# Pinned background sums, gate rows by way of memory, softmax normalization on ScalarE, and value products of two column blocks in one visit

## The chip, the cores and the metric

The kernel runs on one core of a Trainium2 chip. The metric is the device time of one execution in microseconds (us). The core has five engines that the profile tells apart: PE (TensorE, the matmuls, with the weight loads PEld that overlap them), DVE (VectorE), ACT (ScalarE), POOL (GpSimd) and SP (SyncE, which here only issues DMAs). Each engine works through its own queue of instructions in order and waits at an instruction until what that needs is there.

## The reference

Two layers of a diffusion backbone, for 1024 latent tokens of a 16 x 64 grid and 256 context tokens, width 1024. One input projection feeds three branches; their outputs are joined, projected, gated and normalized.

```python
shift, scale, gate = split(silu(c) @ w_mod + b_mod, 3)     # and the same for the context, from c_ctx
h = x * (1 + scale) + shift
p = h @ w_in                                               # cut into rk rv nk nv rq rg nq ng ch cb ccg cz
y = concat([conv(ch, cb, ccg, cz),                         # 4 groups, width-3 filter
            retention(rq, rk, rv) * silu(rg),              # 6 heads x 64, both directions
            neighbourhood(nq, nk, nv) * silu(ng)]) @ w_out # 6 heads x 64
x = layer_norm(ALPHA * x + gate * y)
# neighbourhood, for one latent query: a window of 8 rows x 16 columns and all 256 context keys
s = concat([q . k_window + bias, q . k_ctx]);  o = softmax(s) @ [v_window, v_ctx]
```

Context queries see context keys only, and layer 1 has no context queries.

## The kernel before

**Numbers.** Projections are made in two parts: a tensor is cut into a rounded part and a rest (tiles wh and wl of the weights, h of the activations; KS holds both parts of the keys, QH and QL are the query's), and PE multiplies the parts that matter. All such products go through the helper mm at L86, transposes through L140.

**The order of the work.** PE's order is written out by the program. A class Order keeps a clock od.t, to which every matmul adds its cost; generators that run beside the main line (the attention of a column block, the background sums, the load of the output weights) yield a number and are resumed when the clock has gone on by that much, between two matmuls of a projection. The other engines' orders are made by a scheduler from what each instruction needs and from its priority, which is its place in the program; `behind(60)` (L206) puts the background sums 60 places back, but the scheduler may still put them ahead of an instruction recorded earlier if that one's data come later.

**The background sums.** Mod.background (L189 to L227) makes the modulation's shift, scale and gate columns for later use: tiles wm of w_mod come in by DMA (SP), DVE multiplies them by silu(c) and adds them up in acc (L210 the first, L212 the others, two versions: latent and context), PE transposes acc, DVE sums the transposed columns and adds the bias into the table `tab` (L183). In layer 0 it makes that layer's gate (four groups of columns) and then the shift and scale of layer 1 (eight); in layer 1 only that layer's gate. The job is called `aside` and runs beside the attention branch.

**The attention branch** goes in three column blocks of two heads (p = 0, 1, 2) in each layer, six cores in all. For each, the keys are projected (ps_pj, evacuated into KS by ACT at L659 and by DVE at L660, the rest), POOL builds bias tables B (L715, L720), the queries are projected, and then the generator core (L726 to L817) runs beside the next projections. An item is 128 queries of one head: 4 context items (layer 0 only) and 16 latent ones for each core. One step of the loop at L788 does three things for three different items:

- scores of item `step`: PE makes them into one or two ps_s banks; DVE takes the maximum of the context part (m, L753), adds the bias B and takes the joint maximum (mx, L756), and negates it (nm, L758); ACT takes the exponential with the row sum (L760); DVE forms the reciprocal (L696) and multiplies P by it and by 0.5 (L697, normalize).
- values of an item pair at `step - LAG - 2` (LAG = 2): the two heads' PT tiles times the values VA into ps_pv (L777 to L780), a stretch of matmuls that read 128 rows and write 64 partitions, which the profile shows as tile shape 128*64 while the rest runs as 128*128. This happens at every second step; four of these blocks of 64 columns fill the one ps_pv bank, and ACT copies it out to oN (L808, L810).
- turn of the item at `step - LAG` (L764 to L775): PE transposes its P into ps_pt, ACT copies 512 columns out to PT (L770) and DVE the last 128 (L774).

```python
for step in range(n + LAG + 3):
    if step < n:
        Ps[kind, i] = s_lat(i) if kind == "l" else s_ctx(i)
    back = step - LAG - 2
    if 0 <= back < n and items[back][1] % 2 == 1:
        pv(ov[:, c * 128:(c + 1) * 128], vals, pair)
    back = step - LAG
    if 0 <= back < n:
        PTs[kind, i] = turn(Ps.pop((kind, i)), nt)
    yield (1800 if p < 2 else 1500) if step < n else 800
```

PSUM has eight banks: 3 for ps_pj, 2 for ps_s, 2 for ps_pt and 1 for ps_pv. There are three buffers each for P and PT.

**The end of a layer.** After the third core, w_out (L1070) loads the output weights (SP, 16 loads, L1080) and splits them (ACT L1081, DVE L1082). The gate is a column table (128 partitions), but is needed as a row in every partition: gate_rows (L1050) multiplies the identity by table columns into dg (DVE, L1055) and multiplies dg by a matrix of ones on PE into two ps_s banks; gate_copy (L1064) copies these to gt (ACT, L1067). That happens once for the latent tokens in each layer, and once more for the context in layer 0, beside the sixth tile of the output loop (L1110).

Of the kernel before, what the change touches and what calls it, by code (L numbers as in the profile page):

```python
# [30 lines left out]
LAG = 2  # L31
# [48 lines left out]
def backbone(ctx: ExitStack, tc: tile.TileContext, io):  # L80
# [43 lines left out]
    ones = const.tile([128, 128], F, name="c_ones")  # L124
    dve.memset(ones, 1.0)
# [19 lines left out]
    class Mod:  # L145
# [43 lines left out]
        def background(self, blocks, tmp):  # L189
# [10 lines left out]
            for i, (blk, kk) in enumerate(todo):  # L200
                if i + 2 < len(todo):
                    tiles.append(load(*todo[i + 2]))
# [3 lines left out]
                with behind(60):  # L206
                    for v in range(2):
                        c = cs[:, kk, v:v + 1]
                        if kk == 0:
                            dve.tensor_scalar(acc[:, v], t, c, None, ALU.mult)  # L210
                        else:
                            dve.scalar_tensor_tensor(acc[:, v], t, c, acc[:, v],  # L212
                                                     ALU.mult, ALU.add)
# [415 lines left out]
    def natten_conv(l, h, yT, vn, ctx_q, aside, w_out):  # L629
# [3 lines left out]
        with ExitStack() as st:  # L633
# [60 lines left out]
            def normalize(P, n, s):  # L694
                r = col("rc1")
                dve.reciprocal(r, s)  # L696
                dve.tensor_scalar(P[:, :n], P[:, :n], r, 0.5, ALU.mult, ALU.mult)  # L697
# [28 lines left out]
            def core(p, QH, QL, KS, bias, oN):  # L726
# [37 lines left out]
                def turn(P, nt):  # L764
                    PT = np_.tile([128, 640], F, tag="PT", bufs=3, name="PT")
# [4 lines left out]
                    act.copy(PT[:, :n], pt[:, :n])  # L770
                    if nt > 4:
                        pt = ps_t()
                        transpose(pt[:, :128], P[:, 512:640])
                        dve.tensor_copy(PT[:, 512:640], pt[:, :128])  # L774
# [13 lines left out]
                for step in range(n + LAG + 3):  # L788
# [5 lines left out]
                    back = step - LAG - 2  # L794
                    if 0 <= back < n and items[back][1] % 2 == 1:
                        kind, i = items[back]
                        k = i // 2
                        pair = [PTs.pop((kind, i - 1)), PTs.pop((kind, i))]
                        vals = [VA[:, a, :] for a in (8, 9)]
                        if kind == "l":  # L800
                            k0, nt = window(k)
                            vals += [VA[:, a, :] for a in range(k0, k0 + nt)]
                        c = k % 4
                        if c == 0:
                            ov = ps_v()
                        pv(ov[:, c * 128:(c + 1) * 128], vals, pair)
                        if kind == "c" and k == 1:
                            act.copy(oN[:, SEQ:TOK], ov[:, :256])  # L808
                        elif kind == "l" and c == 3:
# [224 lines left out]
    for l in range(DEPTH):  # L1034
        last = l == DEPTH - 1
        yT = dram.tile([DM, TOK], F, name=f"yT{l}")
        vn = [dram.tile([TOK, 128], F, name=f"vn{l}{p}") for p in range(3)]
        mod_l = mod
        mod_n = None if last else Mod(l + 1)

        def aside(tmp):
            yield from mod_l.background(range(16, 24, 2), tmp)
            if mod_n is not None:
# [3 lines left out]
        with ExitStack() as st:  # L1047
            wo, held, op, job = [], [], None, None

            def gate_rows(v, held):  # L1050

                for hf in range(2):
                    ps = ps_s()
                    dg = const.tile([128, 512], F, tag="m2", name="dg")
                    dve.tensor_tensor(  # L1055
                        dg.rearrange("p (j c) -> p j c", c=128),
                        ident.unsqueeze(1).to_broadcast([128, 4, 128]),
                        mod_l.tab[:, 16 + 4 * hf:20 + 4 * hf, v:v + 1]
                        .to_broadcast([128, 4, 128]), ALU.mult)
                    yield 8000  # L1060
                    mm(ps, ones, dg, True, True, 866)
                    held.append(ps)

            def gate_copy(held):  # L1064
                gt = op.tile([128, DM], F, tag="gt", name="gt")
# [185 lines left out]
```

## Time and profile before

| | us |
|---|---|
| median of 3 runs | 1394.04 (1393.85 to 1395.64) |
| the profiled execution | 1394.43 |
| its span, first to last instruction | 1392.7 |
| PE busy in it (PEld 1161.9) | 1360.6, 98% |
| DVE busy | 945.5, 68% |
| ACT busy | 475.9, 34% |
| POOL busy | 320.4, 23% |

The granted TensorE clock is 0.997 of full speed over the whole span. The profile holds a page (busy time of each engine, the span in slices, the chain of work that ended last, the costliest groups of instructions) and a trace from which rows can be asked: the waits of an engine, the timeline of a stretch, busy time in windows. A row of the timeline gives the start, the duration, the engine, the program's line, the operation, out<-in by tile names, shapes, and how many like instructions it stands for; in square brackets the idle time ahead of it and who ended that. PE records are kept for a part of a long product at times as one, so counts of PE rows ("shown matmuls") are those of the trace.

### The profile page before, as it was taken

The page shows a single profiled execution, that of the slowest core. Times are in us where ns is not written, and L with a number is a line of the kernel's source. Part 1 is how long each engine was busy: PE and PEld are TensorE (multiplying, and loading weights), DVE is VectorE, ACT ScalarE, POOL GpSimd, SP SyncE. Part 2 cuts the span into 40 slices and gives each one's busy share as a digit, 9 for nine tenths or more (in the row PEclk, how much of TensorE's full clock was granted, in tenths as well). Part 3 has the DMA queues.
Part 4 walks back from the last instruction along what each step waited for, and adds up shares of the span by engine and source line. Part 5 has one row for each costly group of instructions (what it writes and reads, how often), then busy time and mean ns, then how long its engine had stood idle before and what let it go on. Part 6 is the DMA issues. An engine that isn't in the chain of part 4 may idle for free.

```text
span 1392.7 us, 23906 instructions
## 1 busy us (share of the span) xinstructions
PE 1360.6 (98%) x9040; PEld 1161.9 (83%) x9040; DVE 945.5 (68%) x2331; ACT 475.9 (34%) x1000; POOL 320.4 (23%) x266
## 2 busy tenths in 40 slices
PE   6999999998999999999999999999999999999997
PEld 4888989887888888888888888888878888887886
DVE  4766473638887877875988766565489756465686
ACT  2422122223453443543344422121234435354210
POOL 1505041341021121000444404041440213100121
PEclk9999999999999999999999999999999999999999
DMA  9720201233113224126343211111252211203642
GB/s 291 225 58 16 58 24 33 71 108 112 54 58 121 86 63 126 43 82 215 133 133 117 83 49 33 48 34 55 69 152 61 74 56 46 80 24 98 197 153 89
DMA packets 160788, 126.31 MB, mean 91 GB/s; under 512 B 10272, under 2 KB 146080, under 8 KB 160672
## 3 DMA queue, kind: packets, MB, share of 16 engines
q1 hardware_dynamic: 160672, 124.78, 29.6%
q8 instruction: 71, 1.16, 0.3%
q14 instruction: 45, 0.37, 0.1%
HBM read 102.98 MB, written 21.76 MB: 90 GB/s over the span
## 4 chain that ended last, share of the span: by engine, by line
PE 86%; DVE 7%; DMA 2%; issue 2%; SPq 1%; ACT 1%; POOL 0%; POOLq 0%; DVEq 0%; ACTq 0%
PE ps_pj L86 66%; PE ps_s L86 7%; PE ps_pt L140 7%; PE ps_pv L86 6%; DVE acc L212 2%; DMA wm<-in_w_mod 2%; PE ps_pt L86 1%; DVE P L756 1%; DVE P L697 1%; DVE KS L660 0%; DVE P L753 0%; DVE sm L424 0%; SPq L157 0%; DMA rs<-in_ropes 0%; DVE rsw L397 0%
## 5 line engine op out<-in xcount | busy, mean ns | idle before, releaser
L86 PE MATMUL ps_pj<-h,wh 128*128 128x512 f32 (+1 forms) x2128 | 624.7, 373 | 6.7 <-DVE KS L660 4.6
L86 PEld LDWEIGHTS ps_pj<-h,wh 128*128 128x128 f32 x2128 | 379.3, 189 | 68.0 <-issue 7.0
L86 PE MATMUL ps_pj<-h,wl 128*128 128x512 f32 (+1 forms) x1064 | 395.6, 372 | 0.0
L86 PEld LDWEIGHTS ps_pj<-h,wl 128*128 128x128 f32 x1064 | 201.5, 189 | 32.1 <-issue 2.9
L86 PE MATMUL ps_pj<-wo,yh 128*128 128x512 f32 (+1 forms) x608 | 182.7, 382 | 0.0
L86 PE MATMUL ps_pj<-wh,h 128*128 128x256 f32 x960 | 175.2, 284 | 1.3 <-ACT nv L430 1.3
L86 PEld LDWEIGHTS ps_pj<-wh,h 128*128 128x128 f32 x960 | 150.5, 192 | 2.0 <-ACT nv L430 1.5
L86 PE MATMUL ps_pj<-wl,h 128*128 128x256 f32 x480 | 136.4, 284 | 0.0
L86 PEld LDWEIGHTS ps_pj<-wo,yh 128*128 128x128 f32 x608 | 112.0, 188 | 21.7 <-issue 1.0
L212 DVE SCALAR_TENSOR_TENSOR acc<-wm,c_silu,acc 128x256 f32<-128x256 f32 x224 | 117.5, 563 | 2.6 <-DMA wm<-in_w_mod 2.2
L86 PE MATMUL ps_pj<-wo,yl 128*128 128x512 f32 (+1 forms) x304 | 115.9, 381 | 0.0
L235 POOL TENSOR_TENSOR wl<-wr,wh 128x512 fp32r<-128x512 f32 x32 | 43.1, 1346 | 313.0 <-ACT wh L243 267.6
L243 ACT CAST wh<-wr 128x512 fp32r<-128x512 f32 x128 | 79.1, 619 | 91.2 <-PE ps_pj L86 86.9
L760 ACT ACTIVATE P<-P,nm 128x640 f32<-128x640 f32 (+1 forms) x96 | 77.3, 805 | 75.4 <-DVE nm L758 72.4
L235 DVE TENSOR_TENSOR wl<-wr,wh 128x512 fp32r<-128x512 f32 x96 | 71.3, 745 | 43.9 <-ACT wh L243 42.6
L770 ACT COPY PT<-ps_pt 128x512 f32<-128x512 f32 (+1 forms) x108 | 60.6, 561 | 101.7 <-PE ps_pt L140 101.3
L86 PEld LDWEIGHTS ps_pj<-wl,h 128*128 128x128 f32 x480 | 92.1, 192 | 0.3 <-POOL wl L235 0.2
L715 POOL TENSOR_TENSOR B<-E,c_rmask 128x256 f32<-128x256 f32 (+1 forms) x36 | 38.4, 1076 | 178.5 <-DVE mx L756 136.7
L140 PE MATMUL ps_pt<-c_ident,P 128*128 128x128 f32 x480 | 73.0, 278 | 1.7 <-DVE P L697 1.1
L422 DVE TENSOR_REDUCE sm<-ps_pj 128x2 f32<-128x128 f32 x60 | 17.3, 289 | 75.6 <-PE ps_pj L86 75.0
L86 PEld LDWEIGHTS ps_pj<-wo,yl 128*128 128x128 f32 x304 | 57.3, 188 | 11.1 <-issue 0.5
L140 PEld LDWEIGHTS ps_pt<-c_ident,P 128*128 128x128 f32 x480 | 54.5, 140 | 12.2 <-issue 7.2
(168 smaller groups left out, 2003.1 us busy)
## 6 DMA issues: line engine op xcount, KB each, us to landing
wr<-in_w_in SPq DMA_DIRECT2D x104, 256.0 KB
wm<-in_w_mod SPq DMA_DIRECT2D x128, 128.0 KB
wr<-yT SPq DMA_DIRECT2D x36, 256.0 KB
yT<-ystage SPq DMA_DIRECT2D x32, 256.0 KB
wr<-in_w_out SPq DMA_DIRECT2D x32, 256.0 KB
wm<-in_w_mod SPq DMA_DIRECT2D x12, 512.0 KB
wr<-in_w_in SPq DMA_DIRECT2D x48, 128.0 KB
z<-in_x SPq DMA_DIRECT2D x8, 512.0 KB
```

The lines of the kernel that those rows point to most:

```text
L86: pe.matmul(out, lhsT, rhs, start=start, stop=stop)
L140: pe.transpose(out, in_, ident[:in_.shape[0], :in_.shape[0]])
L212: dve.scalar_tensor_tensor(acc[:, v], t, c, acc[:, v], ALU.mult, ALU.add)
L235: eng.tensor_tensor(lo, raw, f32(hi), ALU.subtract)
L243: act.copy(hi, raw)
L422: dve.tensor_reduce(sm, ps[:, :128].rearrange("p (h d) -> p h d", d=HD), AX.X, ALU.add)
L697: dve.tensor_scalar(P[:, :n], P[:, :n], r, 0.5, ALU.mult, ALU.mult)
L715: pool.tensor_tensor(B, bass.AP(tensor=E.tensor, offset=E[:, o:o + 1].offset, ap=[list(E.ap[0]), [1, nc_], [RPB_W, 16]]), rmask.unsqueeze( ...
L756: dve.tensor_tensor_reduce(P[:, 256:256 + n], sl[:, :n], B, 1.0, m0, ALU.add, ALU.max, mx)
L760: act.activation(P[:, :256 + n], P[:, :256 + n], AF.Exp, bias=nm, accum_out=s)
L770: act.copy(PT[:, :n], pt[:, :n])
```

## The change

Four edits are made.

1. The sums of the background (L210, L212) are pinned: the scheduler keeps each in its place of the program on DVE, so that it goes behind all DVE instructions recorded ahead of it.
2. The gate rows no longer go over PE. When the gate table is complete, SP writes its columns to a tensor gd in DRAM (one DMA of 128 x 8 single elements for each version) and later reads it back with a broadcast to 128 partitions (one DMA of 512 KB each). The products with ones, dg, the copies and the matrix of ones go. The first broadcast stands ahead of the loads of the output weights, the second (layer 0) ahead of the output loop.
3. The normalization's product moves from DVE to ACT (a Copy with the reciprocal as scale). The factor 0.5 moves to the two evacuations of the transposes.
4. The products with the values are made for two blocks of columns in one stretch, at every fourth step, and one step after the last turn of the four items and not two. PT has four buffers, and a core is two steps shorter.

```diff
-    ones = const.tile([128, 128], F, name="c_ones")
-    dve.memset(ones, 1.0)
...
                         if kk == 0:
-                            dve.tensor_scalar(acc[:, v], t, c, None, ALU.mult)
+                            i = dve.tensor_scalar(acc[:, v], t, c, None, ALU.mult)
                         else:
-                            dve.scalar_tensor_tensor(acc[:, v], t, c, acc[:, v],
-                                                     ALU.mult, ALU.add)
+                            i = dve.scalar_tensor_tensor(acc[:, v], t, c, acc[:, v],
+                                                         ALU.mult, ALU.add)
+                        tc.keep_in_program_order(i)
...
                 r = col("rc1")
                 dve.reciprocal(r, s)
-                dve.tensor_scalar(P[:, :n], P[:, :n], r, 0.5, ALU.mult, ALU.mult)
+                act.activation(P[:, :n], P[:, :n], AF.Copy, scale=r)
...
-                    PT = np_.tile([128, 640], F, tag="PT", bufs=3, name="PT")
+                    PT = np_.tile([128, 640], F, tag="PT", bufs=4, name="PT")
...
-                    act.copy(PT[:, :n], pt[:, :n])
+                    act.activation(PT[:, :n], pt[:, :n], AF.Copy, scale=0.5)
...
-                        dve.tensor_copy(PT[:, 512:640], pt[:, :128])
+                        dve.tensor_scalar(PT[:, 512:640], pt[:, :128], 0.5, None, ALU.mult)
...
-                for step in range(n + LAG + 3):
+                for step in range(n + LAG + 1):
...
-                    back = step - LAG - 2
-                    if 0 <= back < n and items[back][1] % 2 == 1:
-                        kind, i = items[back]
-                        k = i // 2
-                        pair = [PTs.pop((kind, i - 1)), PTs.pop((kind, i))]
...
-                        pv(ov[:, c * 128:(c + 1) * 128], vals, pair)
-                        if kind == "c" and k == 1:
+                    back = step - LAG - 1
+                    if 0 <= back < n and back % 4 == 3:
+                        for x in (back - 3, back - 1):
+                            kind, i = items[x]
+                            k = i // 2
+                            pair = [PTs.pop((kind, i)), PTs.pop((kind, i + 1))]
...
+                            pv(ov[:, c * 128:(c + 1) * 128], vals, pair)
+                        if kind == "c":
...
+        gd = dram.tile([2, DM], F, name=f"gd{l}")
...
             yield from mod_l.background(range(16, 24, 2), tmp)
+            for v in range(1 if last else 2):
+                sp.dma_start(gd[v].rearrange("(b p) -> p b", p=128), mod_l.tab[:, 16:24, v])
             if mod_n is not None:
...
-            def gate_rows(v, held):
-                for hf in range(2):
-                    ps = ps_s()
-                    dg = const.tile([128, 512], F, tag="m2", name="dg")
-                    dve.tensor_tensor(
...
-                    yield 8000
-                    mm(ps, ones, dg, True, True, 866)
-                    held.append(ps)
-            def gate_copy(held):
-                gt = op.tile([128, DM], F, tag="gt", name="gt")
-                for hf, ps in enumerate(held):
-                    act.copy(gt[:, hf * 512:(hf + 1) * 512], ps)
+            def gate_rows(pool, v):
+                gt = pool.tile([128, DM], F, tag="gt", bufs=1, name="gt")
+                sp.dma_start(gt, gd[v:v + 1, :].to_broadcast([128, DM]))
                 return gt
...
-                job = od.start(gate_rows(0, held))
+                gts.append(gate_rows(op, 0))
...
-            od.finish(job)
-            gt = gate_copy(held)
+            if not last:
+                gts.append(gate_rows(lp, 1))
             for t in range(8 if last else 10):
-                if t == 6 and not last:
-                    held = []
-                    job = od.start(gate_rows(1, held))
-                if t == 8:
-                    od.finish(job)
-                    gt = gate_copy(held)
+                gt = gts[t // 8]
```

The instructions on PE go from 7978 to 7972, on DVE from 2309 to 2194, on ACT from 894 to 996; SP issues 580 in place of 574.

On PE, layer 0, second column block, this is one of the steps with a visit to the values before (PT the transposed P, VA the values, c_ident the identity of the transposes); such a step is every second one:

```order
L86 MATMUL ps_s<-KS,QH 128x256
L86 MATMUL ps_s<-KS,QL 128x256
L86 MATMUL ps_s<-KS,QH 128x384
L86 MATMUL ps_s<-KS,QL 128x384
L86 MATMUL ps_pv<-PT,VA 64x128 x10
L140 MATMUL ps_pt<-c_ident,P 128x128 x5
```

The same place now, where such a step is every fourth one:

```order
L86 MATMUL ps_s<-KS,QH 128x256
L86 MATMUL ps_s<-KS,QL 128x256
L86 MATMUL ps_s<-KS,QH 128x384
L86 MATMUL ps_s<-KS,QL 128x384
L86 MATMUL ps_pv<-PT,VA 64x128 x20
L138 MATMUL ps_pt<-c_ident,P 128x128 x5
```

The stretch of value products has become twice as long and stands at half as many places, between the same neighbours; over the program there are 54 before and 27 now.

On ACT, layer 0, first column block, before (L760 the exponential, L770 the copy of the transposes, L659 the evacuation of the next keys, L810 the copy of ps_pv):

```order
L760 ACTIVATE P,sa<-P,nm 128x640
L770 COPY PT<-ps_pt 128x512
L760 ACTIVATE P,sa<-P,nm 128x640
L770 COPY PT<-ps_pt 128x512
L760 ACTIVATE P,sa<-P,nm 128x640
L659 CAST KS<-ps_pj 64x64x8
L810 COPY oN<-ps_pv 128x16x32
L770 COPY PT<-ps_pt 128x512
L760 ACTIVATE P,sa<-P,nm 128x640
L659 CAST KS<-ps_pj 64x64x8
L770 COPY PT<-ps_pt 128x512
```

The same place now, in the line numbers of the changed kernel (L759 the exponential, L696 the new product, L769 the copy, L658 the keys; rc is the reciprocal):

```order
L759 ACTIVATE P,sa<-P,nm 128x640
L696 ACTIVATE P<-P,rc_4278 128x640
L759 ACTIVATE P,sa<-P,nm 128x640
L810 COPY oN<-ps_pv 128x16x32
L696 ACTIVATE P<-P,rc_4315 128x640
L769 ACTIVATE PT<-ps_pt 128x512
L658 CAST KS<-ps_pj 64x64x8
L769 ACTIVATE PT<-ps_pt 128x512
L658 CAST KS<-ps_pj 64x64x8
L759 ACTIVATE P,sa<-P,nm 128x640
L696 ACTIVATE P<-P,rc_4384 128x640
L769 ACTIVATE PT<-ps_pt 128x512
```

A product follows each exponential in ACT's queue, at times with another instruction between, and the copies of the transposes and the casts of the keys stand behind it.

On DVE, layer 0, the first key projection, before (L660 the rest of the keys, two for each bank of ps_pj; L210 and L212 the sums):

```order
L660 TENSOR_TENSOR KS<-ps_pj,KS 64x64x8 x2
L210 TENSOR_SCALAR acc<-wm,c_silu 128x256 x2
L212 SCALAR_TENSOR_TENSOR acc<-wm,c_silu,acc 128x256 x6
L660 TENSOR_TENSOR KS<-ps_pj,KS 64x64x8
L212 SCALAR_TENSOR_TENSOR acc<-wm,c_silu,acc 128x256 x2
L660 TENSOR_TENSOR KS<-ps_pj,KS 64x64x8
L212 SCALAR_TENSOR_TENSOR acc<-wm,c_silu,acc 128x256 x2
```

The same place now (L659 the rest of the keys, L208 and L210 the sums):

```order
L659 TENSOR_TENSOR KS<-ps_pj,KS 64x64x8 x2
L208 TENSOR_SCALAR acc<-wm,c_silu 128x256 x2
L210 SCALAR_TENSOR_TENSOR acc<-wm,c_silu,acc 128x256 x6
L659 TENSOR_TENSOR KS<-ps_pj,KS 64x64x8 x2
L210 SCALAR_TENSOR_TENSOR acc<-wm,c_silu,acc 128x256 x2
L659 TENSOR_TENSOR KS<-ps_pj,KS 64x256
L210 SCALAR_TENSOR_TENSOR acc<-wm,c_silu,acc 128x256 x2
```

Eight sums still stand between the first bank's keys and the second's; the two that stood between the halves of the second bank stand behind them now.

## What the change will do to the time

> **What bounds the kernel now.** I read the page first: busy time by engine, then the chain that ended last.
>
> ```profile
> PE 1360.6 (98%) x9040; PEld 1161.9 (83%) x9040; DVE 945.5 (68%) x2331; ACT 475.9 (34%) x1000; POOL 320.4 (23%) x266
> PE 86%; DVE 7%; DMA 2%; issue 2%; SPq 1%; ACT 1%; POOL 0%; POOLq 0%; DVEq 0%; ACTq 0%
> ```
>
> PE is busy for 1360.6 of the span's 1392.7 us and holds 86% of the chain; only 32.1 us are idle. So there are two places to win: instructions that leave PE's stream, which count in full, and the idle time in which PE waits for another engine. The waits of PE tell what the second can be worth.
>
> ```profile
> PE ps_pv L86 <- DMA wm<-in_w_mod: 8.2, 6, 4.8
> PE ps_pj L86 <- DVE KS L660: 4.6, 2, 3.6
> PE ps_s L86 <- DVE m L753: 2.0, 2, 1.0
> PE ps_s L86 <- DVE mx L756: 1.9, 5, 0.6
> PE ps_pt L140 <- DVE P L697: 1.1, 1, 1.1
> PE ps_pt L140 <- DVE nm L758: 0.3, 1, 0.3
> PE ps_pt L140 <- DVE PT L774: 0.3, 1, 0.3
> ```
>
> The columns are total, times and longest, in us. The first row belongs to the kernel's first stage, which the diff leaves alone. The second is the key projection in which the background sums begin, 4.6 us. The other five lie in the attention stage and have one cause, a late VectorE: 2.0 + 1.9 + 1.1 + 0.3 + 0.3 = 5.6 us. Three windows out of the six attention cores (three column blocks in each layer) say why: one with sums in layer 0, one with sums and one without in layer 1. The columns used are window, length, then busy us of PE, PEld, DVE and ACT.
>
> ```profile
> 345.00:415.00 70.00, 68.87 (x523) 59.51 (x521) 59.53 (x191) 34.34 (x74) 10.82 (x10) 1.00 0.20 59
> 1040.00:1104.00 64.00, 61.40 (x436) 51.53 (x438) 59.75 (x183) 30.47 (x63) 11.06 (x10) 1.00 0.22 64
> 1216.00:1272.00 56.00, 55.63 (x410) 46.69 (x409) 34.91 (x128) 27.96 (x58) 2.85 (x2) 1.00 0.08 23
> ```
>
> Where background sums run beside the softmax, DVE is busy 85% (59.53 of 70.00) and 93% (59.75 of 64.00), and PE loses 1.1 and 2.6 us; ACT stands at 48 to 50%. Without sums (last row) DVE is at 62% and PE loses 0.4.
>
> **The change part by part.** *Visits to the 64-column shape.* The matmuls with the values (tiles PT and VA) run as 128*64, everything around them as 128*128. Two neighbourhoods of PE's timeline price one visit (start, length, and xcount), one without and one with it.
>
> ```profile
> 481.21 0.34 PE L86 MATMUL ps_s<-KS,QL 128*128 128x384 f32 x1
> 481.39 0.71 PE L140 MATMUL ps_pt<-c_ident,P 128*128 128x128 f32 x5
> 481.86 0.48 PE L86 MATMUL ps_pj<-h,wh 128*128 128x256 f32 x2
> ```
>
> ```profile
> 484.45 0.34 PE L86 MATMUL ps_s<-KS,QL 128*128 128x384 f32 x1
> 484.72 1.31 PE L86 MATMUL ps_pv<-PT,VA 128*64 128x128 f32 x20
> 485.96 0.77 PE L140 MATMUL ps_pt<-c_ident,P 128*128 128x128 f32 x5
> 486.48 0.71 PE L86 MATMUL ps_pj<-h,wh 128*128 128x512 f32 x2
> ```
>
> A short visit, of 8 matmuls, gives the pitch:
>
> ```profile
> 462.38 0.66 PE L86 MATMUL ps_pv<-PT,VA 128*64 128x128 f32 x8
> ```
>
> Without a visit PE goes from the last score matmul to the projection in 481.86 - 481.21 = 0.65 us; with one, in 486.48 - 484.45 = 2.03. Of the 1.38 between them the 20 matmuls themselves take 20 x 0.054 = 1.08 (pitch: (1.31 - 0.66) / 12, from the runs of 20 and 8). The visit as such costs 0.30 us. The order has 54 visits before (10 in each of layer 0's three cores, 8 in layer 1's) and 27 now, with the same matmuls: 27 x 0.30 = 8.1 us off PE. A block of the two costs nothing more for coming second, since within a visit the pitch is even.
>
> *The gate rows.* Six products with a matrix of ones, each shown as two matmuls, leave PE. One of them, with the rhythm of the same projection just ahead of it:
>
> ```profile
> 641.08 0.40 PE L86 MATMUL ps_pj<-h,wh 128*128 128x256 f32 x2
> 641.31 0.28 PE L86 MATMUL ps_pj<-h,wl 128*128 128x256 f32 x1
> 641.43 0.40 PE L86 MATMUL ps_pj<-h,wh 128*128 128x256 f32 x2
> 641.67 1.02 PE L86 MATMUL ps_s<-dg,c_ones 128*128 128x512 f32 x2
> 642.13 0.68 PE L86 MATMUL ps_pj<-h,wl 128*128 128x256 f32 x1
> 642.65 0.40 PE L86 MATMUL ps_pj<-h,wh 128*128 128x256 f32 x2
> ```
>
> A group of three takes 641.43 - 641.08 = 0.35; with the gate's two it takes 642.65 - 641.43 = 1.22. So 6 x 0.87 = 5.2 us. In their place SP issues three writes of 1024 single elements to memory and three broadcasts of 512 KB. The writes stand right behind the last gate table's sum, the first broadcast ahead of most loads of the output weights. I cost them at nothing: SP holds 1% of the chain, and weights are loaded ahead. Were that cover gone, the weight loads queued behind the write on SP would be late by its wait for the table, and PE with them once in each layer: up to 2 us, kept for the range.
>
> *Pinned sums.* On DVE the sums no longer overtake what was recorded ahead of them. The two key projections show what that is worth. DVE in layer 0:
>
> ```profile
> 311.75 1.76 DVE L210 TENSOR_SCALAR acc<-wm,c_silu 128x256 f32<-128x256 f32 x2 [1.10 <-DMA wm<-in_w_mod]
> 313.43 6.86 DVE L212 SCALAR_TENSOR_TENSOR acc<-wm,c_silu,acc 128x256 f32<-128x256 f32 x6
> 320.32 0.68 DVE L660 TENSOR_TENSOR KS<-ps_pj,KS 64x512 fp32r<-64x512 f32 x1
> 321.04 0.88 DVE L212 SCALAR_TENSOR_TENSOR acc<-wm,c_silu,acc 128x256 f32<-128x256 f32 x2
> 321.95 0.69 DVE L660 TENSOR_TENSOR KS<-ps_pj,KS 64x512 fp32r<-64x512 f32 x1
> ```
>
> The matmul on PE that waits for it, and POOL's work of the same time:
>
> ```profile
> 322.79 0.70 PE L86 MATMUL ps_pj<-h,wh 128*128 128x512 f32 x2 [3.63 <-DVE KS L660]
> ```
>
> ```profile
> 314.17 3.45 POOL L715 TENSOR_TENSOR B<-E,c_rmask 128x256 f32<-128x256 f32 x3
> ```
>
> PE's bank comes free with the fourth KS, at 321.95 + 0.69. The new order still has eight sums ahead of the third KS, but none between third and fourth: it gains 321.95 - 320.32 - 0.68 = 0.95 us here and, the order being the same, in layer 1: 1.9 us of the 4.6. The rest stays: the six sums take 6.86 / 6 = 1.14 us each, most of it while POOL builds its tables, against 0.88 / 2 = 0.44 right after, and both the six and the tables stand where they stood. If a new order brought them to 0.44, they would end 4.2 us earlier, the whole 4.6 would go, and the sum below would be 18.7 in place of 16.0; I don't take it, since nothing is moved between the six and the tables. [...]
>
> *Normalization on ScalarE.* DVE loses 108 products, ACT gains them.
>
> ```profile
> L697 DVE TENSOR_SCALAR P<-P,rc 128x640 f32<-128x640 f32 x72 | 41.7, 579 | 1.0
> L760 ACT ACTIVATE P<-P,nm 128x640 f32<-128x640 f32 x72 | 59.9, 832 | 48.5 <-DVE nm L758 45.6 <-PE ps_pt L140 1.8 <-DVE rc L696 0.2
> ```
>
> DVE gives up 41.7 us in the 72 long ones alone, 12 a core and so 7 us in each window: from 85 and 93% to 75 and 82%, or less with the short ones. No row shows the product on ACT; the nearest is the exponential of the same tile on the same engine, 0.832 us for 640 columns. The bounds are 0.58 (DVE's) and 0.83; I take 0.83. ACT's new load is about 16 x 0.83 = 13 us a core, which lifts 48 to 50% to some 67 to 70%. The halving goes into the copies out of PSUM (L770, L774) as a factor and costs nothing there; the lost gate copies and the lost memset are hidden anyway. What can come of it: the 5.6 us of late VectorE shrink, between all of it (5.6) and nothing; I take half, 2.8, since at 62% load a core still lost 0.4. And there is a new wait: ACT stands idle at the product until DVE's reciprocal is done, and behind it in its queue stand the copy of the transposes and casts for the projections. PE waits for that copy, for it needs the PSUM bank at the next transposes and the copy at the next visit. The margin, from one item whose product is this one, and whose transposes are those at 485.96:
>
> ```profile
> 481.84 0.55 DVE L697 TENSOR_SCALAR P<-P,rc 128x640 f32<-128x640 f32 x1
> ```
>
> The product ends at 482.39, which leaves 3.6 us, against 0.3 us more for the product and one hand-over from DVE to ACT. So most items are covered. A first item of a core, or one behind a group of sums, is not; nearest is the 2.0 us that PE waits now for m. Bounds of the new waits: 0 and 27 visits x 0.5 = 13.5; I take 2.0. The transposes are turned a step nearer to their product (one step, not two), with a fourth PT buffer; the copy at 0.6 us has a step of over 3 us, so this is at nothing.
>
> *The sum.* 8.1 + 5.2 + 1.9 + 2.8 - 2.0 = 16.0 us. The profiled execution took 1394.43 us, 0.39 over the median of the runs, so 1394.43 - 16.0 = 1378.4 in its terms and 1394.04 - 16.0 = 1378.0 in the median's.
>
> **The rivals.** *VectorE's waits all go and ACT adds none.* Then 8.1 + 5.2 + 1.9 + 5.6 = 20.8 us: 1373.2. For it: DVE's load falls by a tenth of each window. Against it: that the last window still loses something at 62%.
>
> *ACT gives half of it back.* In a visit's step the queue has exponential, product, copy; if the copy is late by 0.3 us at each of the 27 visits, 8.1 us are lost on top of the 2.0 left out: 1378.0 + 8.1 - 2.0 = 1384.1. For it: ACT waits 45.6 us for nm even now, so it follows DVE closely. Against it: the 3.6 us of margin.
>
> *The visits do not merge.* If the price of a visit sits in each block and not in the change of shape, the 8.1 stay: 1386.1. Against it stand the even pitch and the eight matmuls that cost the same at either end.
>
> *Slower: ACT becomes what PE waits for.* If the copy in the visit's step comes behind a whole product that PE has to see out, 0.83 us at each of 27 visits is 22.4 us against a gain of 18.0: 1394.0 + 4.4 = 1398.4. It decides from 18.0 / 27 = 0.67 us a visit on. [...]
>
> **How the numbers follow.** The forecast 1378.0 has 0.55; its own range goes from the first rival's 1373.2 to 1378.0 + 2.8 + 2.0 = 1382.8 (no wait of VectorE goes, and the weights come late); waits all gone 0.20; half given back 0.12; visits not merged 0.03; slower 0.06; about no change 0.04. No change means within 0.2%, 2.8 us, about what a measurement of this kernel can tell. Faster is 0.55 + 0.20 + 0.12 + 0.03 = 0.90. The range goes from 1371.0 (the first rival less the 2 us by which a key wait may shrink further) to 1387.0 (past the third rival), leaving out the slower cases and a little below.
>
> **What would show it.** In the profile after: 27 visits of 8 to 40 shown matmuls with the 0.30 gone at the others; no ps_s<-dg; PE's busy time down by about 13; PE's waits for KS about 2.7; the five VectorE rows together near 2.8; new rows of PE ps_pt or ps_pv waiting for ACT PT near 2.0; ACT at 65 to 72% in the cores. Waits for ACT above 10 us would make it wrong upward; no waits for ACT and under 1 us for DVE, downward.

## The result, and the profile after

| | before | changed |
|---|---|---|
| median, us | 1394.52 (1393.85 to 1395.64, 4 runs) | 1384.47 (1380.88 to 1386.18, 4 runs) |
| ratio of the times, 95% interval | | 0.9922 [0.991, 0.9934] |
| profiled execution, us (span) | 1394.43 (1392.7) | 1380.88 (1379.1) |

The change makes the kernel 10.05 us faster, clear of the 0.2% that the prediction counts as no change. The forecast was 1378.0 with a range of 1371.0 to 1387.0; the median lies in the range, 6.5 us above the forecast. The changed kernel's runs spread over 5.3 us, and those of before over 5.4 in the later comparisons (1392.23 to 1397.63, 29 runs); where that comes from is a finding of its own.

The page after: busy time by engine and the chain.

```profile
PE 1346.2 (98%) x9028; PEld 1159.9 (84%) x9028; DVE 895.4 (65%) x2216; ACT 550.4 (40%) x1102; POOL 321.5 (23%) x266
PE 85%; DVE 7%; DMA 3%; issue 2%; ACT 1%; SPq 1%; POOL 0%; POOLq 0%; DVEq 0%; ACTq 0%
```

PE's busy time has fallen by 14.4 us, the span by 13.6: nothing was won in PE's idle time as a whole, though almost every single wait has changed. The waits of PE after:

```profile
PE ps_pv L86 <- DMA wm<-in_w_mod: 6.4, 5, 4.8
PE ps_pj L86 <- DVE KS L659: 3.9, 2, 3.3
PE ps_pt L138 <- ACT P L696: 3.0, 3, 1.5
PE ps_pj L86 <- ACT wh L242: 2.1, 1, 2.1
PE ps_pj L86 <- POOL wl L234: 1.8, 1, 1.8
PE ps_pj L86 <- ACT yh L242: 1.4, 1, 1.4
PE ps_pt L138 <- issue: 1.4, 1, 1.4
PE ps_pt L138 <- ACT PT L769: 1.0, 2, 0.7
PE ps_pj L86 <- ACT nv L429: 0.7, 1, 0.7
PE ps_s L86 <- DVE mx L755: 0.7, 2, 0.4
PE ps_pv L138 <- ACT m L169: 0.5, 1, 0.5
PE ps_pt L138 <- DVE ht L964: 0.3, 1, 0.3
```

The five rows of a late VectorE (5.6 us) have shrunk to one of 0.7 us for mx. In their place stand 3.0 + 1.0 us for ScalarE's product and copy, and two waits that before did not have: 1.4 us for yh, the first input of layer 1's output projection, and 1.4 us, put down to "issue", in layer 0's output loop. In the first stage, which the change leaves alone, PE waits 1.8 us less for wm and 1.8 us more for wl; both change from run to run.

A visit of PE to the values in the changed kernel, with the score matmul ahead and the projection behind:

```profile
484.59 0.34 PE L86 MATMUL ps_s<-KS,QL 128*128 128x384 f32 x1
484.86 2.40 PE L86 MATMUL ps_pv<-PT,VA 128*64 128x128 f32 x40
487.20 0.76 PE L138 MATMUL ps_pt<-c_ident,P 128*128 128x128 f32 x5
487.72 0.47 PE L86 MATMUL ps_pj<-h,wl 128*128 128x512 f32 x1
```

From score to projection it takes 3.13 us for 40 matmuls. Less 0.65 without a visit and 40 x 0.054, there remain 0.32 us: the price does not grow with the matmuls of a visit, and two blocks pay it once. ScalarE's product and its load in the first core:

```profile
L696 ACT ACTIVATE P<-P,rc 128x640 f32<-128x640 f32 x72 | 59.8, 830 | 19.1 <-DVE rc L695 18.9
```

```profile
342.00:412.00 70.00, 68.73 (x539) 60.93 (x539) 55.98 (x180) 48.29 (x96) 10.46 (x10) 1.00 0.21 61
```

0.830 us for 640 columns, as taken; ACT is at 69% (48.29 of 70.00), DVE at 80%.

**PE's clock.** The runs' spread and a part of the difference go with the granted clock. This is the stretch at the first key projection before, cut where the clock changed, with as long a stretch ahead (columns: window, length, then busy us of PE, PEld, DVE, ACT, POOL, then PEclk):

```profile
319.96:323.37 3.41, 0.58 (x3) 0.52 (x4) 3.28 (x7) 1.56 (x3) 0.05 (x1) 1.00 0.46 127
323.37:326.79 3.42, 3.42 (x10) 2.65 (x9) 3.26 (x9) 1.56 (x4) 0.00 (x0) 0.50 0.37 108
```

In the window in which PE waits for KS it is busy for 0.58 of 3.41 us; in the next 3.42 us its clock is 0.50, and three products (wh, wh, wl) take 1.28 us there (from 323.69) for 0.70 right behind (from 327.20). By the clock 3.42 x 0.50 = 1.7 us are lost; this estimate is what a halved window is counted at below. The same place in the profiled execution of the changed kernel, in two windows of that length:

```profile
317.55:320.96 3.41, 1.87 (x16) 1.66 (x14) 3.38 (x4) 0.00 (x0) 2.72 (x3) 1.00 0.14 38
320.96:324.38 3.42, 1.63 (x7) 1.42 (x8) 2.68 (x6) 1.93 (x4) 0.00 (x0) 1.00 0.39 115
```

The wait is nearly as long (3.3 us for 3.6). PE is busy for 1.87 us of the one window and 1.63 of the other, and the clock stays at 1.00 there and in the 3.41 us behind. This execution has no halved window at all before PE's last matmul (1.00 from the start to 1370.67 us), and is the fastest of the four runs (clock 0.999; the others show 0.995). So of the 13.55 us between the two profiled executions 1.7 are a halved window that only the one of before has, and 11.9 are the change.

### The profile page after: what moved, and what is told of

It reads as the page before. It is cut to its first block, busy times and chain, and to the rows that moved or that the text cites. A ratio compares the mean times of both kernels' runs of the same rounds, so it can differ in the third digit from the quotient of the medians.

```text
span 1379.1 us, 23747 instructions
## 1 busy us (share of the span) xinstructions
PE 1346.2 (98%) x9028; PEld 1159.9 (84%) x9028; DVE 895.4 (65%) x2216; ACT 550.4 (40%) x1102; POOL 321.5 (23%) x266
## 4 chain that ended last, share of the span: by engine, by line
PE 85%; DVE 7%; DMA 3%; issue 2%; ACT 1%; SPq 1%; POOL 0%; POOLq 0%; DVEq 0%; ACTq 0%
PE ps_pj L86 65%; PE ps_s L86 6%; PE ps_pt L138 6%; PE ps_pv L86 6%; DMA wm<-in_w_mod 2%; DVE acc L210 2%; DMA wr<-in_w_out 1%; PE ps_pt L86 1%; DVE KS L659 1%; DVE P L755 0%; DVE acc L208 0%; DVE sm L423 0%; DVE wl L234 0%; SPq L155 0%; ACT P L759 0%
## 5 line engine op out<-in xcount | busy, mean ns | idle before, releaser
L210 DVE SCALAR_TENSOR_TENSOR acc<-wm,c_silu,acc 128x256 f32<-128x256 f32 x224 | 117.9, 565 | 6.7 <-DMA wm<-in_w_mod 5.8
L759 ACT ACTIVATE P<-P,nm 128x640 f32<-128x640 f32 (+1 forms) x96 | 77.1, 803 | 44.6 <-DVE nm L757 42.5
L696 ACT ACTIVATE P<-P,rc 128x640 f32<-128x640 f32 (+2 forms) x108 | 83.2, 771 | 27.3 <-DVE rc L695 27.2
L769 ACT ACTIVATE PT<-ps_pt 128x512 f32<-128x512 f32 (+1 forms) x108 | 61.3, 568 | 29.9 <-PE ps_pt L138 28.5
```

The costliest lines, as they stand in the source:

```text
L210: i = dve.scalar_tensor_tensor(acc[:, v], t, c, acc[:, v], ALU.mult, ALU.add)
L696: act.activation(P[:, :n], P[:, :n], AF.Copy, scale=r)
L759: act.activation(P[:, :256 + n], P[:, :256 + n], AF.Exp, bias=nm, accum_out=s)
L769: act.activation(PT[:, :n], pt[:, :n], AF.Copy, scale=0.5)
```

## The experiments

All are timed against the kernel before on the same chip; its medians there were 1394.99, 1395.32 and 1395.33.

**The gate rows alone.** Before, with this part of the change's diff:

```diff
-                job = od.start(gate_rows(0, held))
+                gts.append(gate_rows(op, 0))
...
-            gt = gate_copy(held)
+            if not last:
+                gts.append(gate_rows(lp, 1))
```

> Only the gate rows by way of memory, all else as before. My theory: PE loses six products at 0.87 us each, 5.2 us, and the DMAs cost nothing: about 1389.3 against 1394.5. Rival (weights late): the output weights stand behind the gate's DMAs on SP, PE waits about 2 us more at the start of an output projection in each layer: about 1393. On the spread: if the spread of the changed kernel (1380.9 to 1386.2) comes from stretches in which PE's clock is halved after a long wait of PE at the key projection, this kernel, which has that wait (3.6 us), can show it too, and its slow runs have the lower clock; if it comes from the product on ACT, this kernel has none of it.

Measured: 1394.99, ratio 1.0002 [0.9993, 1.0011]: no gain, and the theory's 1389.3 is missed. Its page and its largest new wait:

```profile
PE 1357.3 (97%) x9028; PEld 1160.6 (83%) x9028; DVE 938.1 (67%) x2324; ACT 474.0 (34%) x994; POOL 321.8 (23%) x266
```

```profile
PE ps_pj L86 <- ACT yh L241: 3.5, 1, 3.5
```

PE's busy time fell by 3.3 us with one halved window more in it than before (granted clock 0.996 for 0.997), so by 5.0 without: the products did leave. But PE then waits 3.5 us at the start of layer 1's output, and a halved window follows: 3.5 + 1.7 = 5.2 us, all of the gain. The rival had one place right, but not what makes the wait, as the next run shows. The eleven runs spread over 5.4 us, so a spread like that of the changed kernel doesn't need the product on ACT. Between the last value product of layer 1 and the first output product lie 25.1 us before and 26.9 here, although two of the products (1.7 us) are gone from there.

**The gate alone, with one more buffer.**

```diff
-        return wring.tile([128, 512], F, tag="wr", bufs=3, name="wr")
+        return wring.tile([128, 512], F, tag="wr", bufs=4, name="wr")
```

> The gate by way of memory alone, with four buffers for the raw weights and outputs in place of three. With three, PE waits 3.5 us for the first yh of layer 1's output, and the gate alone gains nothing. Theory (the ring): the two products with ones had only filled PE's time while the loads of the output weights went round the three buffers, some 3 us each; with a fourth the wait falls under 1 us, the halved window after it goes, and the kernel comes to 1389 to 1391. Rival (the broadcast delays the loads, or memory is slow): the wait stays at 2 us or more, 1393 to 1395.

Measured: 1389.36, ratio 0.9961 [0.9949, 0.9974], 6.0 us faster. The wait for yh is gone from the list, no halved window stands there (granted clock 0.997 for 0.996 with three buffers), and the 26.9 us are 23.2. So in that stage the three buffers set the end: with three, each load of the output weights takes 2.8 to 4.3 us from issue to cast, and the output weights and the first inputs go through the same ring. That the products with ones had filled PE's time there fits this, but is argued. The extra buffer without the gate's edit wasn't tried, so how much of the 6.0 us it would bring by itself stays open.

**The gate and the visits.** The gate's edit and the loop with two blocks and four PT buffers; the product on DVE, no pinning.

```diff
-                    back = step - LAG - 2
-                    if 0 <= back < n and items[back][1] % 2 == 1:
+                    back = step - LAG - 1
+                    if 0 <= back < n and back % 4 == 3:
+                        for x in (back - 3, back - 1):
```

> The gate rows by way of memory and the values in visits of two column blocks with four PT buffers; the product stays on DVE, the sums are not pinned. My theory: 27 visits less at 0.30 us, 8.1 us below the kernel with the gate alone, 13.3 below before: about 1381. Rival (the price sits in each block and not in the visit): no gain over the gate alone, about 1389. If this kernel comes out at or below the whole change (1384.5), the product on ACT and the pinning bring nothing together.

Measured: 1398.41, ratio 1.0029 [1.0018, 1.0039]: 3.4 us slower than before, and both expectations missed. Its largest new wait, with the row of one such wait and two windows around it:

```profile
PE ps_pt L138 <- DVE P L695: 8.5, 4, 3.0
```

```profile
413.54 0.65 PE L138 MATMUL ps_pt<-c_ident,P 128*128 128x128 f32 x4 [2.36 <-DVE P L695]
```

```profile
411.60:415.01 3.41, 1.48 (x9) 1.18 (x9) 1.81 (x5) 1.85 (x6) 0.00 (x0) 1.00 0.38 115
415.01:418.43 3.42, 3.42 (x31) 3.18 (x32) 1.41 (x4) 0.95 (x3) 0.00 (x0) 0.50 0.00 1
```

The waits stand at the ends of the cores. There the steps follow each other closely (yield 800), and before, a visit stood between the last scores and the last transposes; with visits at every fourth step none does, and PE reaches the transposes ahead of the product. In the window with this wait of 2.36 us PE is busy for 1.48 of 3.41 us, and in the next the clock is 0.50. This execution has five halved windows, 8.5 us: at the keys, at three ends of cores and at the output; its granted clock is 0.992, for 0.997 before.

**The normalization alone.**

```diff
-                dve.tensor_scalar(P[:, :n], P[:, :n], r, 0.5, ALU.mult, ALU.mult)
+                act.activation(P[:, :n], P[:, :n], AF.Copy, scale=r)
```

> Only the normalization's product on ACT, with the factor 0.5 in the copies. My theory: PE's waits for DVE in attention (5.6 us) go to under 1.5 and waits for ACT of about 4 us take their place: within 2 us of before, 1392 to 1395. Rival (ACT jitter): the new waits for ACT change from run to run and this kernel is slower than before by 3 to 5 us in most runs, with the spread of the whole change and no difference in the clock. Second rival (prediction's first): all of DVE's waits go and ACT adds none, 1389.

Measured: 1392.13, ratio 0.9977 [0.9969, 0.9986], 2.9 us faster, spread 2.2 us. The waits in attention:

```profile
PE ps_s L86 <- DVE mx L756: 1.3, 4, 0.5
PE ps_pt L140 <- ACT P L697: 1.0, 1, 1.0
PE ps_pt L140 <- DVE PT L774: 0.6, 1, 0.6
```

5.6 us have become 2.9. The time stands at the low end of the 1392 to 1395 expected: of the 4 us of waits for ACT that the theory added only 1.0 came, in a kernel whose visits still stand at the cores' ends. The rival that ACT makes the runs uneven fell.

**The pinning alone.**

```diff
+                        tc.keep_in_program_order(i)
```

> Only the pinned sums. My theory: the pair of sums that goes behind the keys had filled the time in which DVE waits for ACT's cast, so each key projection gains 0.3 to 0.4 us and not 0.95: 0.7 us in all, no change that can be told, 1393 to 1394.5. The prediction's term was 1.9. Rival: sums that may not overtake make DVE stand idle in attention, where it is 85 to 93% busy, and cost 1 us or more: over 1395.5.

Measured: 1394.84, ratio 1.0000 [0.9991, 1.0008]. PE's wait for KS is 4.2 us for 4.6. In attention its waits changed places without shrinking: two of 0.8 us each, behind the sums' own instructions on DVE (acc and msum), are new, so the rival has a part too.

**The whole change without the normalization.** The diff of the normalization alone, turned round, in the changed kernel.

> The whole change with the normalization's product back on DVE (the factor 0.5 too). Theory A (the product on ACT is what makes the two-block visits pay): at a core's end no visit stands any more between the last scores and the last transposes, DVE's product comes late there (8.5 us of PE's waits, up to 3.0 each, in the kernel with visits and gate), and PE's clock is halved for 3.4 us after most of them: 1396 to 1399, though the sums are pinned here. Theory B (what made it late were sums that overtook the product): pinning alone mends it, 1385 to 1389, and the waits of PE for P are under 3 us.

Measured: 1397.31, ratio 1.0011 [1.0001, 1.0020]. Theory A holds (granted clock 0.995 in the profiled run, for 0.999 of the changed kernel's); theory B falls, although the waits for P are 6.2 us for the 8.5 without pinning:

```profile
PE ps_pt L138 <- DVE P L696: 6.2, 4, 2.4
```

The product on ACT is worth 2.9 us alone and some 12 in the whole change (1397.31 against 1384.47, less 0.8 by which the kernels before beside them differ: 1395.32 and 1394.52). In this run a window in which PE is busy for 1.56 of 3.41 us is followed by one at a clock of 1.00:

```profile
1101.80:1105.21 3.41, 1.56 (x10) 1.12 (x10) 3.32 (x9) 2.11 (x5) 0.27 (x1) 1.00 0.38 115
1105.21:1108.63 3.42, 3.42 (x43) 3.03 (x43) 2.87 (x7) 0.59 (x1) 0.00 (x0) 1.00 0.14 44
```

**The whole change without the visits.** The old loop in the changed kernel, with three PT buffers.

> The whole change with the visits of one column block each, as before (three PT buffers, two steps more). Theory: 27 visits more cost 8.1 us, and the cover they give at a core's end takes some 2 us of waits away: 1389 to 1391. If the visits were worth nothing even with the product on ACT, it would be 1384 to 1385.

Measured: 1388.64, ratio 0.9954 [0.9940, 0.9967], just under the theory's 1389 to 1391; the whole change on the same chip 1384.26. The two-block visits are worth 4.4 us of time (the two intervals just touch). Their price in PE's work is larger; the first line is the kernel without the visits:

```profile
PE 1356.6 (98%) x9028; PEld 1160.6 (84%) x9028; DVE 898.4 (65%) x2216; ACT 548.5 (40%) x1102; POOL 322.2 (23%) x266
```

and this the whole change in the same comparison:

```profile
PE 1347.4 (97%) x9028; PEld 1161.2 (84%) x9028; DVE 894.0 (65%) x2216; ACT 550.4 (40%) x1102; POOL 321.0 (23%) x266
```

9.2 us less, of which 1.7 are a halved window more in the former (granted clock 0.996 for 0.997): 7.5 us, 0.28 a visit. Of them PE gives back 3.0 at the ends of the cores (waits for P, none with the old visits).

**The whole change again.**

> The changed kernel again, for more runs and a second trace. [...] So the runs lie between 1380.9 (none, as in the first trace) and about 1380.9 + 4 x 1.7 = 1387.7, the trace shows one to three halved windows inside the span, and its time is 1380.9 plus 1.7 for each, to within 1 us. Rival (waits change from run to run): the waits summed differ by 3 us or more from the first trace and explain the time without the clock.

Measured: 1384.26, ratio 0.9927 [0.9913, 0.9941], runs from 1382.79 to 1386.91. The trace, of a run of 1383.95, has one halved window, behind the wait for KS (granted clock 0.997 for 0.999). By the expectation this makes 1380.88 + 1.7 = 1382.6; it is 1.4 more, so the bound of 1 us was missed. The rest is in the waits: yh 2.1 for 1.4, "issue" 2.0 for 1.4, KS 4.3 for 3.9, nv 1.3 for 0.7, the first stage's loads 1.0 more, against 1.4 less for wl: 1.9 in sum, under the 3 us that the rival asked for. So both have a part, 1.7 us the clock and 1.4 the waits. The four windows at the upper end of the expected range are the author's estimate; the runs end at 1386.91, at clocks from 0.994 to 0.997.

**Later tables.** In the changed kernel the first bias tables of a layer are recorded behind the first keys.

```diff
-            bias = tables(0)
             keys(0)
+            bias = tables(0)
```

> The whole change with POOL's first bias tables of each layer recorded behind the first key projection, so that the first sums don't run beside them. Theory: the six sums take 0.44 to 0.5 us each and not 1.14, PE's wait for KS (3.9 us) falls under 1, and the halved stretch of 1.7 us that follows it when the wait falls into one grid window goes too: 1379 to 1381, no run at a clock below the profiled one's by that wait. Rival (the sums' slowness is not POOL's): 1384.5, the wait stays. Second rival: the tables come late for the first scores or slow the queries' casts, and PE waits there as much: 1384 to 1386.

Measured: 1376.30 (1375.36 to 1377.61), ratio 0.9863 [0.9850, 0.9876]; 8 us better than the whole change, and more than the theory's 1379 to 1381. VectorE at the first keys, and POOL:

```profile
311.81 2.46 DVE L210 SCALAR_TENSOR_TENSOR acc<-wm,c_silu,acc 128x256 f32<-128x256 f32 x6
315.16 0.69 DVE L659 TENSOR_TENSOR KS<-ps_pj,KS 64x512 fp32r<-64x512 f32 x1 [0.89 <-ACT KS L658]
317.12 0.69 DVE L659 TENSOR_TENSOR KS<-ps_pj,KS 64x512 fp32r<-64x512 f32 x1 [1.27 <-ACT KS L658]
317.84 2.49 DVE L210 SCALAR_TENSOR_TENSOR acc<-wm,c_silu,acc 128x256 f32<-128x256 f32 x2
```

```profile
313.85 3.19 POOL L714 TENSOR_TENSOR B<-E,c_rmask 128x256 f32<-128x256 f32 x3 [4.60 <-DMA E<-in_rpb]
```

The six sums, nearly all done before the tables begin, take 2.46 / 6 = 0.41 us each; the two that run beside them 2.49 / 2 = 1.25. The edit does a second thing: on SP the sums' tiles wm now go ahead of the tables' inputs E, so the six sums start 2.1 us behind the first key's KS for 4.8 in the changed kernel. They end 7.1 us earlier, 4.4 by their speed and 2.7 by their start; the run doesn't part the two. PE's wait for KS is gone from the list, and so is the halved window (granted clock 0.998): from the first key cast to the first scores it takes 25.8 us for 30.8 in the trace of the whole change run again (0.997), where both stand; in layer 1 it takes 22.9 for 24.0. That a wait has to fall into one window of a grid to be followed by a halved stretch, as the expectation has it, is not shown.

**Wider ends of the cores.**

```diff
-                    yield (1800 if p < 2 else 1500) if step < n else 800
+                    yield 1800 if p < 2 else 1500 if step < n else 800
```

> The whole change with the last three steps of a core spaced like the others in the first two column blocks (1800 for 800), so that the last transposes come later behind their product. Theory: the 3.0 us that PE waits for P from ACT fall under 1.5, the halvings that follow them in some runs go with them: 1381 to 1383 against 1384.5, and a narrower spread. Rival: the ends of the cores cost nothing beyond what the profile shows and the later end makes the gate's products wait: 1384 to 1386.

Measured: 1382.41 (1380.60 to 1382.82), ratio 0.9903 [0.9888, 0.9917]. PE's wait for P falls from 3.0 to 0.3 us:

```profile
PE ps_pt L138 <- ACT P L696: 0.3, 1, 0.3
```

The time fell by about 2 us, but its interval overlaps that of the whole change, so this run alone doesn't show the gain. That halved stretches go with the wait is not shown: the granted clock of the four runs is 0.994 to 0.996, for 0.994 to 0.999 in the changed kernel's nine.

**A later broadcast of the latent gate.** The broadcast of gt is held behind the first two loads of the output loop.

```diff
-                sp.dma_start(gt, gd[v:v + 1, :].to_broadcast([128, DM]))
+                if v:
+                    sp.dma_start(gt, gd[v:v + 1, :].to_broadcast([128, DM]))
...
+                if t == 0:
+                    tc.keep_in_program_order(
+                        sp.dma_start(gt, gd[0:1, :].to_broadcast([128, DM])))
```

> The whole change with the latent gate's broadcast of 512 KB issued behind the first two loads of the output loop and not ahead of the output weights. Theory: the weights come 1 to 2 us earlier in layer 1, PE's wait for yh (1.4 us in the profiled run, 3.5 with the gate alone) goes, and with it a halving in some runs: 1381.5 to 1383.5. Rival: the weights were late for another reason, or the first product with the gate now waits for it: 1384.5 to 1386.

Measured: 1387.26 (1382.89 to 1388.17), ratio 0.9933 [0.9921, 0.9945]: the theory fell. The wait for yh is 1.6 us for 1.4 to 2.1, so the broadcast ahead of the weights had not made it. What the run showed instead is the other new wait, of PE for the first transposes of z in layer 0's output loop, 2.4 us here. VectorE's row of that place, in this kernel, in the changed kernel and before:

```profile
664.37 1.30 DVE L1127 SCALAR_TENSOR_TENSOR z<-z,lt 128x512 f32<-128x512 f32 x2 [7.50 <-DMA z<-in_x]
```

```profile
659.13 1.29 DVE L1123 SCALAR_TENSOR_TENSOR z<-z,lt 128x512 f32<-128x512 f32 x2 [6.46 <-DMA z<-in_x]
```

```profile
662.19 0.69 DVE L1139 SCALAR_TENSOR_TENSOR z<-z,lt 128x512 f32<-128x512 f32 x1 [4.10 <-DMA z<-in_x]
```

On SP the broadcast of the context gate, 512 KB, stands right ahead of the loads of z, and VectorE waits 2.4 us longer for z in the changed kernel than before (6.46 for 4.10). From the issue of the first z to its use it takes 8.5 us there and 7.4 before. With the gate's edit alone the broadcast stands there too (9.9 us), but PE doesn't wait for it.

**Three mends together.** The changed kernel with later tables, wider ends, and the context gate's broadcast recorded at the fifth tile of the output loop.

```diff
-            if not last:
-                gts.append(gate_rows(lp, 1))
...
+                if t == 4 and not last:
+                    gts.append(gate_rows(lp, 1))
```

> The whole change with three edits: POOL's first tables recorded behind the first keys (1376.3 alone), the last steps of a core spaced wider in the first two column blocks (1382.4 alone, against 1384.5), and the context gate's broadcast recorded behind the first loads of the output loop's inputs (its own part: the z that DVE waits for in layer 0, 1.4 us of PE). Theory: 1376.3 less 2 for the ends less 1 to 3 for z with its halved window: 1371.5 to 1374. Rival: the parts overlap, since the later end of a core only moves the wait: 1375 to 1377.

Measured: 1372.11 (1370.39 to 1373.54), ratio 0.9836 [0.9822, 0.9849], as the theory had it. It beats both kernels: 23 us under before, 12 under the change. PE's waits:

```profile
PE ps_pv L86 <- DMA wm<-in_w_mod: 8.1, 6, 4.8
PE ps_pj L86 <- ACT yh L242: 2.7, 1, 2.7
PE ps_pj L86 <- ACT wh L242: 2.1, 1, 2.1
PE ps_pj L86 <- ACT nv L429: 1.3, 1, 1.3
PE ps_pt L138 <- ACT PT L769: 1.0, 2, 0.7
```

KS and "issue" are gone, and P is at 0.2 us. From the issue of the first z to its use it takes 6.4 us. The wait for yh has stayed, as the ring of three buffers would have it; a fourth buffer was not tried in this kernel. The third edit was not run by itself.

## Why the prediction was right, and where it was not

The sign, the range and most mechanisms were right; the sum was 6 us too good. Among its signs, PE's busy time fell by 12.7 us without the halved window, for "about 13", and ACT stands at 69%, for 65 to 72. By its own steps:

- *Visits, 8.1 us.* Right in kind, 7.5 measured in PE's work. The cover was missed: the step "A block of the two costs nothing more for coming second" is true of the matmuls, but the prediction did not ask what the visits that vanish had been standing in front of. At a core's end they were the cover of the last product. That costs 3.0 us with the product on ACT and 6.2 to 8.5 with it on DVE, without the halved windows; so the visits are worth 4.4 us here and make the kernel slower where the product stays on DVE.
- *Gate rows, 5.2 us.* PE's work fell by 5.0, the time by nothing when the edit stood alone. The step that failed is "I cost them at nothing" with its bound of 2 us: in the changed kernel PE waits 1.4 us for z, behind a broadcast (2.4 in the run with the later gt), and the two products in layer 1 stood in a stage that the ring of loads ends, not PE. With the fourth buffer the whole term came (6.0 us).
- *Pinned sums, 1.9 us.* 0.3 to 0.7 measured in PE's wait for KS, 0.0 in time. Of the gap of 0.95 us between two KS only 0.30 was freed. The changed kernel has the third KS and the fourth in these rows,

```profile
320.58 0.68 DVE L659 TENSOR_TENSOR KS<-ps_pj,KS 64x512 fp32r<-64x512 f32 x1
321.91 0.69 DVE L659 TENSOR_TENSOR KS<-ps_pj,KS 64x512 fp32r<-64x512 f32 x1 [0.65 <-ACT KS L658]
```

  with 0.65 us in which DVE waits for ACT's cast, which itself comes behind the third KS. The two sums had filled most of the gap at no cost. That the rest of the 4.6 us comes from sums that are slow beside POOL's tables, as the prediction read its rows, the later tables bear out (1.25 us against 0.41), though there the sums also start earlier. What makes them slow there is not shown.
- *Late VectorE, 2.8 of 5.6 us.* Too small: 4.9 went.
- *New waits for ACT, 2.0 us.* 4.0 in the trace, but not where they were looked for: not at the visits in the middle of a core, where the margin of 3.6 us held. The product's 3.0 lie in the last steps of three cores, and 0.7 of the copy's 1.0 in the last core, at a step without a visit. The product took the 0.83 us that were assumed, and the factor 0.5 made the copies hardly longer (ACT's of 512 columns 0.592 us for 0.584, DVE's 0.286 for 0.287). The rival in which ACT gives half back named nearly the measured time, 1384.1, for a cause that the trace does not show; the slower one did not come. The product itself takes longer on ACT than on DVE (0.830 against 0.579 us), yet the move cuts this kernel's time by 2.9 us alone and some 12 beside the other edits.
- *Not in the sum at all: the halved clock.* The prediction took each wait at its length. Behind the wait of 3.63 us before and the one of 2.36 with the visits and the gate stands a window at a clock of 0.50, 1.7 us more each; behind the one of 3.33 in the changed kernel's first trace none does.

The trace's own account: 7.5 + 5.0 + 0.7 + 4.9 - 4.0 - 1.4 - 1.4 = 11.3 us, against the 11.9 that the two profiled executions differ by without the halved window. The 7.5 and the 5.0 are taken from other runs. The forecast's range held in part by luck: terms that were too large (the gate rows net of their waits, the sums) stood against one too small (the late VectorE).

## What to carry to other kernels

When work leaves the engine that is the bound, ask at each place what comes next there and whether it is ready: a product that is removed or moved may have been the cover of another engine's result, or may stand in a stage that a ring of buffers ends. Edits like these do not add: the same move was worth 2.9 us alone and some 12 beside others. And look at the granted clock behind PE's long waits: here the wait of 3.63 us at the keys had 3.42 us at a clock of 0.50 behind it, and so was worth more than its length.

## What the runs showed of the hardware

In the trace of before PE's clock is 0.50 in one stretch of its work, 3.42 us long, and 1.00 in the rest of it; in the first trace of the changed kernel it is 1.00 up to PE's last matmul. The stretch before stands behind PE's wait of 3.63 us for KS; with the gate and the visits one of 3.42 us at 0.50 (415.01 to 418.43) stands behind a wait of 2.36 us for P. In the changed kernel PE waits 3.33 us for KS, and the clock stays at 1.00. So the length of a wait does not tell by itself whether the clock behind it is halved; what does is not shown.

The granted clocks fit as a cause of the changed kernel's spread: of its nine runs the four at 0.996 or more took 1380.88 to 1384.26 us, the five at 0.994 or 0.995 took 1383.16 to 1386.91. How much of the spread the clock makes is not shown beyond the two traces.

A stretch of products of the 128*64 shape among those of 128*128 costs PE 0.28 to 0.32 us beyond its matmuls: 0.30 with 20 of them before, 0.32 with 40 in the changed kernel, 7.5 / 27 = 0.28 from the run without the visits. That it is the change of shape that costs this is not shown apart. VectorE's multiply-add of 128x256 took 0.41 us with nearly all of it ahead of POOL's additions and 1.25 beside them, in the run with later tables.
